# Weight parts of the token mixer made by converting and accumulating transfers, and the meta keys' rests stacked into one value product

## The chip, the cores and the metric

The kernel runs on one core of one Trainium2 chip, in one launch. The metric is the device time of an execution in microseconds. Engines are called by their names in the profile: PE (TensorE matmul) and PEld (its weight loads), DVE (VectorE), ACT (ScalarE), POOL or Pool (GpSimd), SP (SyncE, which here only issues transfers).

## What is computed

One decoder layer on 512 tokens of width 1024 with 16 meta tokens in front: half a SwiGLU FFN (inner width 2816), a token mixer, another half FFN. The reference, cut to the mixer:

```python
def token_mixer(h, ...):
    qa, ka, va, fa, qb, kb, vb, ga, gb = jnp.split(h @ w_in, idx, axis=-1)
    # qa, ka: rms_norm per head (8 heads of 64); qb 8 heads, kb, vb 2 heads, normed too
    log_f = jax.nn.log_sigmoid(fa + forget_bias)
    o_fox = fox_attention(qa, ka, va, log_f)       # causal, + c_q - c_k with c = cumsum(log_f)
    o_swa = swa_attention(qb, kb, vb, sinks, rel_bias_table)
    # each query block of 128 sees its own block, the block before and the 16 meta keys
    y = sigmoid(ga) * (o_fox @ w_branch_fox) + sigmoid(gb) * (o_swa @ w_branch_swa)
    return y @ w_out
```

## The kernel before

**Products in two parts.** Every fp32 operand of a large product is split into a leading part in fp32r (names ending in H, or `wh`) and the rest (L, or `wl`). `prod` (lines 301 to 304) makes one product of three matmuls: leading by leading, leading by rest, rest by leading.

**Weights.** Weights are read in pieces of 128x1024 (512 KB), in the fixed order of the list `pieces`. `load_to` has SP transfer a piece into a buffer `raw`; `split_to` then has ACT cast it into `wh` (`hi`, line 133) and DVE write the rest `wl = raw - wh` (`lo`, line 140). Each of the names `raw`, `wh`, `wl` has three buffers. `piece()` hands out the next piece; it keeps five pieces loaded ahead and three split ahead. The FFNs and the gates' last part use products with sums of weights instead (pieces of kinds A to D), some of which Pool's accumulating transfers make (line 211, `raw` and `rawC` from `in_w1i`, `in_wg` and others, 256 KB each).

**The mixer** (361.6 to 601 us of the profile). The projection is cut into nine chunks of 256 columns with two pieces each (rows 0 to 511 and 512 to 1023 of the weight): first v of the first four fox heads together with the forget gate, then k, q of the same heads, v, k, q of the other four, then k and v of the sliding window, then its two q chunks. Then come three gate pieces `wg` and four pieces `wbr` of the branch product, another gate piece, and the rest. `tok_chunk` makes a chunk for five token tiles (tile 0 is the 16 meta tokens, whose H and L stand side by side in `xm`, so that lines 1009 and 1010 take two matmuls instead of three). For k and q, `head_norm` takes ACT's squares, DVE's sums and a reciprocal root on Pool (`rsq`, line 351), then DVE scales, PE transposes (line 1139) and ACT and DVE evacuate into `kH`, `kL`, `qH`.

**Attention.** Units of attention are woven between the steps of the chunks that come later, so that PE always has projections to do while DVE and ACT work on a softmax; a scheduler then fixes the order on each engine. A fox unit takes two heads and 256 queries: scores (line 1221) with DVE's pass over them (line 1240), exponentials on ACT (line 1181), transposes (line 1266), evacuation into `pH` and `pL`, and value products (lines 1280 and 1281): for each key tile one matmul with `pH` and one with `pL`. Its stationary side `v` carries the leading part and the rest of v side by side in 128 columns, so one product gives both. Tile 0 of the keys holds the 16 meta keys in rows 0 to 15; rows 16 to 127 of that block of `v` are zero. A sliding-window unit takes four heads and one block of 128 queries: scores with the bias added on DVE (`tensor_tensor_reduce`, L1375 in the profile), exponentials, transposes (line 1388) per key tile, and value products (lines 1399 and 1400). Blocks 1 to 3 have three key tiles there, block 0 two: the meta keys (a tile of 16 rows) and its own block.

Of the kernel before, what the change touches and what calls it, by code (L numbers as in the profile page):

```python
# [41 lines left out]
TH = T // 2  # L42

# [39 lines left out]
def kernel(  # L83
# [117 lines left out]
    state = {"use": 0, "load": 0, "split": 0}  # L201
# [36 lines left out]

    def load_to(n):
        while state["load"] < min(n, holds[0] if holds else n, len(pieces)):  # L240
            c = state["load"]
            state["load"] += 1
            kind, *what = pieces[c]
            if kind == "w":
                parts = what[0]
                nk = parts[0][1]
                w = sum(p[2] for p in parts)
                raw = wp.tile([P, PW], F32, tag="raw", name=nm("raw"))
                rv = raw[:, : nk * w].rearrange("p (k c) -> p k c", c=w)
                c0 = 0  # L250
                for ap, _, n_ in parts:
                    SP.dma_start(rv[:, :, c0 : c0 + n_], ap)
                    c0 += n_
                raws[c] = (raw[:, : nk * w], nk, w)
            elif kind == "A":
                raws[c] = load_first(*what)
            elif kind == "B":
                raws[c], raws[c + 1], raws[c + 2] = load_others(*what)
# [5 lines left out]
    def split_to(n):  # L264
        while state["split"] < min(n, len(pieces)):
            c = state["split"]
            load_to(c + 1)
            state["split"] += 1
            raw = raws.pop(c)
            if callable(raw):  # L270
# [12 lines left out]

    def piece(ahead=None, then=None):

        c = state["use"]
        state["use"] += 1
        if then is not None and c in split:
            then(split[c])
            then = None  # L290
        split_to(c + (ahead or state["ahead"]))
        load_to(c + 5)
        if then is not None:
            then(split[c])
        return split.pop(c)

# [732 lines left out]
    def tok_chunk(alloc, tiles, evac, finish=None):  # L1029
# [3 lines left out]
        def one(i, half):  # L1033
# [45 lines left out]

    def v_evac(v, i, src):  # L1080
# [5 lines left out]
        lo(d[:, :, 1], src, d[:, :, 0], r1[:n, i : i + 1])  # L1086

# [105 lines left out]
    def fox_pair(box, p, ip, before):  # L1193
# [60 lines left out]
        def turn(hh):  # L1254
            for gr in [list(range(j, min(j + 2, nt))) for j in range(0, nt, 2)]:
# [13 lines left out]
                hi(pH[:, a:b], ps[:, a:b])  # L1269
                lo(pL[:, a:b], ps[:, a:b], pH[:, a:b])  # L1270

        def values(hh):
# [3 lines left out]
            for j in range(nt):  # L1276
# [4 lines left out]
                PE.matmul(pv[:, a:256], st, pL[:, c0 + a : c0 + 256], start=False, stop=j == nt - 1)  # L1281
# [65 lines left out]
    def swa_unit(box, qbox, g, i, before):  # L1347
# [6 lines left out]
        tiles = [(0, M, P), (1, P, 0)] if i == 0 else [(i, P, 0), (0, P, P), (i + 1, P, KS)]  # L1354

        def scores():
            before()
            q, k, b1 = qbox["q"], box["k"], b1s[g]
            for hp in range(2):
                t2 = new("t", [P, 546], F32, 4)  # L1360
                for hh in (2 * hp, 2 * hp + 1):
# [10 lines left out]
                        [(0, P, b1[:, hh, KS:]), (P, KS, bm0[:, h])] if i == 0 else [(0, nk, b1[:, hh])]  # L1372
                    )
                    for pi, (a, b, bt) in enumerate(bias):
                        V.tensor_tensor_reduce(  # L1375
                            out=t[:, a:b], in0=ps[:, a:b], in1=bt, scale=-0.125, scalar=init,
# [7 lines left out]
        def turn():  # L1384
            for tt, n, c0 in tiles:
                ps = psum()
                for hh in range(4):
                    PE.transpose(ps[:n, P * hh : P * hh + P], ts_[hh][:, c0 : c0 + n], ident)  # L1388
                pH, pL = new("pH", [P, 512], bufs=3), new("pL", [P, 512], bufs=3)
                hi(pH[:n], ps[:n])  # L1390
                lo(pL[:n], ps[:n], pH[:n])
                pts.append((pH, pL))

        def values():
            v = box["v"]
            pv = psum()
            for j, ((tt, n, c0), (pH, pL)) in enumerate(zip(tiles, pts)):
                st = v[:n, tt, P * g : P * g + P]
                PE.matmul(pv, st, pH[:n], start=j == 0, stop=False)
                PE.matmul(pv, st, pL[:n], start=False, stop=j == len(tiles) - 1)  # L1400
# [8 lines left out]
    def feat_steps(wsrc, srcH, srcL, nk, c0, use, cuts=4, w=S, whole=False):  # L1409
# [3 lines left out]
        def part(j):  # L1413
            if j == 0:
                box["w"] = wsrc()
                box["ps"] = psum(whole)
            wH, wL = box["w"]
# [19 lines left out]
    w0 = [piece(), piece()]  # L1437
    ps0 = [psum() for _ in every]
    for k in range(KD):
        for i in every:  # L1440
# [116 lines left out]
    stM.close()  # L1557

# [361 lines left out]
```

## Time and profile before

| | us |
|---|---|
| median of 3 runs | 1080.73 (1080.53 to 1080.74) |
| span of the profiled execution | 1078.4 |
| first FFN, mixer, rest of the gates and second FFN | 361.6, 239.4, 477.4 |
| busy in the span: PE, PEld | 1069.1 (99%), 1037.1 (96%) |
| busy in the span: DVE, ACT, POOL | 891.8 (83%), 656.5 (61%), 196.2 (18%) |

The profile is one execution; its span runs from the first to the last instruction, and 2.3 us of the run's time lie outside it. Matmuls overlap, so the time that one costs is the distance between the starts of two neighbours and not its own duration. In a row of the timeline stand the start, the duration, engine, line, operation, output<-inputs and shape, and in brackets how long the engine had been idle before it and what ended that.

### The profile page before, as it was taken

What the parts mean: (1) busy time and instruction counts of PE and PEld (TensorE: products, weight loads), DVE (VectorE), ACT (ScalarE), POOL (GpSimd) and SP (SyncE); (2) the same over time, 40 slices, a digit from 0 to 9 for tenths busy, and PEclk for the clock granted to TensorE, in tenths of its full rate; (3) what the DMA queues carried; (4) which work ended last, traced back from release to release, by engine and by line L of the source; (5) the groups of instructions that cost most, each with busy time, mean ns of one, the idle gap of its engine ahead of it and who ended that gap; (6) DMA issues with size and microseconds to landing.
All of it is one profiled execution on the core that took longest, in us unless ns stands there. A gap on an engine that the chain in (4) does not pass through costs nothing.

```text
span 1078.4 us, 22338 instructions
## 1 busy us (share of the span) xinstructions
PE 1069.1 (99%) x8587; PEld 1037.1 (96%) x8587; DVE 891.8 (83%) x1718; ACT 656.5 (61%) x1243; POOL 196.2 (18%) x232
## 2 busy tenths in 40 slices
PE   8999999999999999999999999999999999999998
PEld 8999999999999999999887799999999999999998
DVE  7988878888889577788897799788998788887895
ACT  7667456656666455556667866555666466645664
POOL 3011111121124431221200110001122211221120
PEclk9999999999999999999999999999999999999999
DMA  8787778688776423112211765466688877887753
GB/s 280 199 220 161 191 190 197 153 219 213 183 177 171 121 81 118 54 47 81 80 50 50 234 165 149 172 200 197 175 204 164 201 192 179 178 194 193 161 122 104
DMA packets 111723, 173.06 MB, mean 160 GB/s; under 512 B 10800, under 2 KB 58160, under 8 KB 111232
## 3 DMA queue, kind: packets, MB, share of 16 engines
q1 hardware_dynamic: 74032, 122.03, 35.5%
q0 software_dynamic: 28768, 37.83, 22.7%
q10 hardware_dynamic: 8816, 11.77, 3.4%
q8 instruction: 67, 1.10, 0.4%
q14 instruction: 40, 0.33, 0.1%
HBM read 167.37 MB, written 6.32 MB: 161 GB/s over the span
## 4 chain that ended last, share of the span: by engine, by line
PE 92%; DVE 3%; ACT 3%; issue 1%; DMA 0%; POOL 0%; SPq 0%; ACTq 0%; DVEq 0%
PE ps L301 16%; PE ps L304 15%; PE ps L302 15%; PE pt L301 13%; PE pt L302 13%; PE pt L304 13%; ACT t L1181 1%; ACT wh L133 1%; DVE wl L140 1%; PE pt L1221 1%; PE pt L1266 1%; DMA xt<-in_x_dram 0%; PE ps L1388 0%; DVE t L1184 0%; PE ps L1221 0%
## 5 line engine op out<-in xcount | busy, mean ns | idle before, releaser
L301 PE MATMUL ps<-x,wh 128*128 128x256 f32 (+2 forms) x768 | 219.7, 286 | 0.1
L302 PE MATMUL ps<-x,wh 128*128 128x256 f32 (+2 forms) x768 | 218.9, 285 | 0.5 <-DVE x L142 0.4
L304 PE MATMUL ps<-x,wl 128*128 128x256 f32 (+2 forms) x768 | 218.9, 285 | 0.0
L140 DVE TENSOR_TENSOR wl<-raw,wh 128x1024 fp32r<-128x1024 f32 (+3 forms) x125 | 150.0, 1201 | 44.4 <-ACT wh L133 43.1
L133 ACT CAST wh<-raw 128x1024 fp32r<-128x1024 f32 (+3 forms) x125 | 128.5, 1029 | 88.9 <-PE ps L302 58.3
L301 PEld LDWEIGHTS ps<-x,wh 128*128 128x128 f32 x768 | 144.7, 189 | 1.7 <-ACT hT L686 0.3
L302 PEld LDWEIGHTS ps<-x,wh 128*128 128x128 f32 x768 | 144.5, 188 | 1.4 <-DVE x L142 0.9
L304 PEld LDWEIGHTS ps<-x,wl 128*128 128x128 f32 x768 | 144.6, 188 | 0.8
L301 PE MATMUL pt<-x,wh 128*128 128x256 f32 (+2 forms) x424 | 125.3, 297 | 0.2 <-ACT wh L133 0.2
L304 PE MATMUL pt<-x,wl 128*128 128x256 f32 (+2 forms) x424 | 124.5, 294 | 0.0
L302 PE MATMUL pt<-x,wh 128*128 128x256 f32 (+2 forms) x392 | 112.5, 287 | 0.0
L133 ACT CAST wh<-tc 128x1024 fp32r<-128x1024 f32 (+1 forms) x70 | 71.9, 1026 | 64.5 <-DVE tc L234 57.1
L140 DVE TENSOR_TENSOR wl<-tc,wh 128x1024 fp32r<-128x1024 f32 (+1 forms) x70 | 83.5, 1193 | 32.5 <-ACT wh L133 32.2
L301 PE MATMUL ps<-acts,wh 128*128 128x264 f32 (+1 forms) x352 | 100.5, 285 | 0.1
L304 PE MATMUL ps<-acts,wl 128*128 128x264 f32 (+1 forms) x352 | 99.9, 284 | 0.0
L302 PE MATMUL ps<-acts,wh 128*128 128x264 f32 (+1 forms) x352 | 99.5, 283 | 0.0
L140 DVE TENSOR_TENSOR wl<-rawC,wh 128x1024 fp32r<-128x1024 f32 (+1 forms) x70 | 84.2, 1203 | 5.8 <-ACT wh L133 5.5
L133 ACT CAST wh<-rawC 128x1024 fp32r<-128x1024 f32 (+1 forms) x70 | 71.6, 1023 | 22.8 <-PE pt L302 17.8
L301 PEld LDWEIGHTS pt<-x,wh 128*128 128x128 f32 x424 | 79.9, 189 | 2.6 <-ACT wh L133 0.5
L304 PEld LDWEIGHTS pt<-x,wl 128*128 128x128 f32 x424 | 79.7, 188 | 2.1
L302 PEld LDWEIGHTS pt<-x,wh 128*128 128x128 f32 x392 | 73.8, 188 | 0.6
L301 PEld LDWEIGHTS ps<-acts,wh 128*128 128x128 f32 x352 | 66.5, 189 | 0.7 <-DVE h2T L918 0.3
(424 smaller groups left out, 3251.0 us busy)
## 6 DMA issues: line engine op xcount, KB each, us to landing
rawC<-in_w1i_dram SPq DMA_DIRECT2D x20, 512.0 KB, 4.6
raw<-in_w1i_dram SPq DMA_DIRECT2D x40, 256.0 KB, 4.2
raw<-in_w2i_dram SPq DMA_DIRECT2D x40, 256.0 KB, 3.4
rawC<-in_w2i_dram SPq DMA_DIRECT2D x20, 512.0 KB, 4.4
raw<-in_wm_dram SPq DMA_DIRECT2D x18, 512.0 KB, 4.4
raw<-in_wout_dram SPq DMA_DIRECT2D x16, 512.0 KB, 4.0
rawD<-in_w1i_dram SPq DMA_DIRECT2D x20, 256.0 KB, 4.1
raw<-in_w1i_dram POOLq DMA_DIRECT2D x20, 256.0 KB, 5.1
```

The costliest lines, as they stand in the source:

```text
L133: return A.copy(o, i)
L140: return V.tensor_tensor(out=o, in0=i, in1=h, op=ALU.subtract)
L301: PE.matmul(ps, sH, mH, start=first, stop=False, **more)
L302: PE.matmul(ps, sH, mL, start=False, stop=False, **more)
L304: shared["mm"] = PE.matmul(ps, sL, mH, start=False, stop=last, **more)
L1181: shared["exp"] = A.activation(t, t, AF.Exp, bias=nmx, scale=-1.0, accum_out=l[:, j : j + 1])
L1221: PE.matmul(ps[:, :w], q[qx][hb, hp, P * i : P * i + P], k[kx][hb, hp, c0 : c0 + w], start=qx + kx == 0, stop=qx == 1 and not last,)
L1266: PE.transpose(ps[:, c : c + P], ts_[hh][(c // P) % 2][:, c0 : c0 + P], ident)
```

## The change

**Weights.** 23 pieces become a new kind "m": the sixteen of the chunks behind the first, the first three of `wg` and the four of `wbr[0]`. For these, `load_to` calls `round_by_dma`, a transfer on Pool's queue that converts f32 to fp32r on its way into `wh`. `split_to` calls `rest_by_dma`: ACT writes `wl = -wh`, and a second transfer of the same weights on Pool's queue is added into `wl`. SP no longer loads these pieces, ACT no longer casts them and DVE no longer subtracts. Every fourth such piece takes two `raw` buffers in place of a `wh` and a `wl`. In the mixer, four pieces are loaded and two split ahead, and `pump` starts the second transfers at fixed places in a chunk.

**Meta keys.** Pool copies the meta rows of `v` also into rows 32 to 47 of the same block, and DVE writes the rest of the meta keys' probabilities into rows 32 to 47 of `pH`, so that one value product takes both; the product with `pL` goes for tile 0. The first block of the sliding window takes its meta keys at the front of the tile with its sink column, with 128-row transposes and products as in the other blocks.

```diff
+    def round_by_dma(ap, nk, w):
+
+        tags = ("raw", "raw") if made[0] % 4 == 3 else ("wh", "wl")
+        made[0] += 1
+        wh, wl = (wp.tile([P, PW], F32R, tag=t, name=nm("m" + t)) for t in tags)
+        wh, wl = (t[:, : nk * w].rearrange("p (k c) -> p k c", c=w) for t in (wh, wl))
+        G.dma_start(wh, ap)
+        return ap, wh, wl
+
+    def rest_by_dma(ap, wh, wl):
+
+        A.activation(wl, wh.bitcast(F32), AF.Copy, scale=-1.0)
+        G.dma_start(wl, ap, accum_op=ALU.add)
+        return wh, wl
...
-            pieces.append(("w", [(wm[c][:, k : k + 4, :], 4, 256)]))
+            pieces.append(("w" if c == 4 else "m", [(wm[c][:, k : k + 4, :], 4, 256)]))
-    pieces += [("w", [(wg[m], 8, 128)]) for m in range(NG - 1)]
-    pieces += [("w", [(wbr[0, c], 4, 256)]) for c in range(4)]
+    pieces += [("m", [(wg[m], 8, 128)]) for m in range(NG - 1)]
+    pieces += [("m", [(wbr[0, c], 4, 256)]) for c in range(4)]
...
         split_to(c + (ahead or state["ahead"]))
-        load_to(c + 5)
+        load_to(c + state["room"])
...
+    def pump():
+        split_to(state["use"] + 2)
...
+            if half and i == tiles[1]:
+                pump()
...
+    def meta_rest(p, ps, w):
+
+        lo(p[REST : REST + M, :w], ps[:M, :w], p[:M, :w])
+
...
+        if i == 0:
+            w = d.shape[1] * 2 * HD
+            G.tensor_copy(v[REST : REST + M, 0, :w], v[:M, 0, :w].bitcast(F32))
...
+                if gr[0] == 0:
+                    meta_rest(pH, ps, 256)
+                    a = 256
                 lo(pL[:, a:b], ps[:, a:b], pH[:, a:b])
...
-                PE.matmul(pv[:, a:256], st, pL[:, c0 + a : c0 + 256], start=False, stop=j == nt - 1)
+                if j:
+                    PE.matmul(pv[:, a:256], st, pL[:, c0 + a : c0 + 256], start=False, stop=j == nt - 1)
...
-        tiles = [(0, M, P), (1, P, 0)] if i == 0 else [(i, P, 0), (0, P, P), (i + 1, P, KS)]
+        tiles = [(0, 0), (1, M + 1)] if i == 0 else [(i, 0), (0, P), (i + 1, KS)]
...
     w0 = [piece(), piece()]
+    state.update(mix=True, room=4, ahead=2)
+    load_to(state["use"] + 2)
...
     stM.close()
+    state.update(room=5, ahead=3)
```

In the built program PE has 24 matmul rows fewer, POOL 49 rows more, SP 23 fewer. Line numbers of the rows below are those of the kernel they are from.

POOL at the start of the mixer, before: the last small loads, then memsets of `v` and `qn`, and the reciprocal root for v.

```order
L967 DMA bm0_4863<-biasd_142 128x8x16
L968 DMA gq_4871<-in_gqk_dram 128x4
L969 DMA fb_4872<-in_fbias_dram 128x8
L970 DMA snk_4873<-in_sinks_dram 128x8
L1100 MEMSET v_692_4896 128x512
L1126 MEMSET qn_718_5105 128x256
L1100 MEMSET v_770_5430 128x512
L351 TENSOR_TENSOR r1_4890<-r1_4890,nhalf_83 128x5
```

The same place after the change (`mwh` and `mwl` are the two parts of a piece made by transfers; `mwh_693` with `mwl_694` and `mwh_695` with `mwl_696` are the two pieces of the first k chunk):

```order
L1000 DMA snk_4869<-in_sinks_dram 128x8
L254 DMA mwl_694_4899<-in_wm_dram 128x1024
L1139 MEMSET v_690_4892 128x512
L1165 MEMSET qn_714_5099 128x256
L248 DMA mwh_695_4901<-in_wm_dram 128x1024
L1139 MEMSET v_764_5424 128x512
L254 DMA mwl_696_4902<-in_wm_dram 128x1024
L248 DMA mwh_706_5068<-in_wm_dram 128x1024
L381 TENSOR_TENSOR r1_4886<-r1_4886,nhalf_83 128x5
```

The converting transfer of the second piece now stands behind two memsets, its accumulating one behind a third, and the root behind both and behind the next chunk's first transfer.

ACT around the evacuation of the second fox group's q (`qH`), before: squares for head norms (`hsq`), a cast of a piece, probabilities (`pH`), then `qH`.

```order
L1061 ACTIVATE hsq_946_6283<-pt_938_6242 128x256
L133 CAST wh_953_6310<-raw_892_6020 128x1024
L1094 COPY hsq_949_6297<-ps_948_6290 64x256
L1025 COPY hsq_960_6339<-pt_959_6322 16x256
L133 CAST pH_965_6353<-ps_964_6352 128x512
L133 CAST pH_968_6362<-pt_967_6361 128x512
L1061 ACTIVATE hsq_962_6344<-hsq_960_6339 16x128
L133 CAST pH_971_6371<-ps_970_6370 128x128
L134 ACTIVATE qH_889_6015<-ps_974_6390,gq_4871 128x512
```

And after the change, where L253 is the negating copy:

```order
L1093 ACTIVATE hsq_934_6273<-pt_926_6231 128x256
L1133 COPY hsq_937_6286<-ps_936_6280 64x256
L253 ACTIVATE mwl_883_6014<-mwh_882_6013 128x1024
L1055 COPY hsq_946_6324<-pt_945_6307 16x256
L134 CAST pH_951_6339<-ps_950_6338 128x512
L1093 ACTIVATE hsq_948_6329<-hsq_946_6324 16x128
L134 CAST pH_954_6349<-pt_953_6348 128x512
L134 CAST pH_957_6358<-ps_956_6357 128x128
L253 ACTIVATE mwl_942_6300<-mwh_941_6299 128x1024
L135 ACTIVATE qH_879_6007<-ps_960_6377,gq_4867 128x512
```

One cast ahead of these steps became two negations, one ahead of five of them and one right ahead of `qH`.

More of the change, by code (lines that the diff above doesn't have):

```diff
@@ L42 @@
 TH = T // 2
+REST = 32
 def bc(ap, pos, n):
@@ L200 @@
     xm_place = lambda n: cp.tile([P, KD * P], F32R, tag="xm", name=nm(n))
-    state = {"use": 0, "load": 0, "split": 0}
+    state = {"use": 0, "load": 0, "split": 0, "room": 5, "mix": False}
     shared = {}
@@ L237, in load_others @@
         return sums, (c[:, : 2 * w], 2 * n, 128), (d[:, :w], n, 128)
+    made = [0]
+    def round_by_dma(ap, nk, w):
[9 more added lines that the diff above has]
+        return wh, wl
     def load_to(n):
@@ L241, in load_to @@
             c = state["load"]
+            if pieces[c][0] == "m" and not state["mix"]:
+                return
             state["load"] += 1
             kind, *what = pieces[c]
-            if kind == "w":
+            if kind == "m":
+                raws[c] = round_by_dma(*what[0][0])
+            elif kind == "w":
                 parts = what[0]
@@ L266, in split_to @@
             c = state["split"]
+            if pieces[c][0] == "m" and not state["mix"]:
+                return
             load_to(c + 1)
@@ L269, in split_to @@
             raw = raws.pop(c)
+            if pieces[c][0] == "m":
+                split[c] = rest_by_dma(*raw)
+                continue
             if callable(raw):
@@ L1384, in turn @@
         def turn():
-            for tt, n, c0 in tiles:
+            for tt, c0 in tiles:
                 ps = psum()
                 for hh in range(4):
[L1388 to L1391, printed above, removed]
+                    PE.transpose(ps[:, P * hh : P * hh + P], ts_[hh][:, c0 : c0 + P], ident)
+                pH, pL = new("pH", [P, 512], bufs=3), None
+                hi(pH, ps)
+                if tt:
+                    pL = new("pL", [P, 512], bufs=3)
+                    lo(pL, ps, pH)
+                else:
+                    meta_rest(pH, ps, 512)
                 pts.append((pH, pL))
@@ L1396, in values @@
             pv = psum()
[L1397 to L1400, printed above, removed]
+            for j, ((tt, c0), (pH, pL)) in enumerate(zip(tiles, pts)):
+                st = v[:, tt, P * g : P * g + P]
+                PE.matmul(pv, st, pH, start=j == 0, stop=False)
+                if tt:
+                    PE.matmul(pv, st, pL, start=False, stop=j == len(tiles) - 1)
             pvv = pv.rearrange("p (a b q) -> p a b q", b=2, q=P)
@@ L1416, in part @@
                 box["ps"] = psum(whole)
+            elif j == 1:
+                pump()
             wH, wL = box["w"]
```

8 lines of the change are left out of this document (5 added, 3 removed).

## Prediction

> **What bounds the kernel now.** I read the busy times by stage first (per engine PE, PEld, DVE, ACT, POOL, then clock, DMA share, GB/s; 361.60 to 601.00 us is the mixer, the stretch that the change touches), then the chain of waits by engine.
>
> ```profile
> 361.60:601.00 239.40, 237.26 (x1819) 216.02 (x1818) 186.00 (x536) 141.59 (x342) 41.68 (x57) 1.00 0.24 75
> 601.00:1078.40 477.40, 473.19 (x3855) 465.56 (x3853) 401.01 (x674) 287.91 (x500) 77.52 (x79) 1.00 0.71 179
> sum 1078.40, PE 1069.13 PEld 1037.10 DVE 891.80 ACT 656.50 POOL 196.18; mean PE 356.38 PEld 345.70 DVE 297.27 ACT 218.83 POOL 65.39
> ```
>
> ```profile
> PE 92%; DVE 3%; ACT 3%; issue 1%; DMA 0%; POOL 0%; SPq 0%; ACTq 0%; DVEq 0%
> ```
>
> PE is busy for 1069 of 1078.4 us and carries 92% of the chain; in the mixer it is idle for 239.40 - 237.26 = 2.1 us, at a full clock (1.00). So there are two ways to move the time: fewer matmuls (a gain at once), or a new wait of PE (a loss at once, since there is hardly any idle time to absorb it). DVE (186.0 of 239.4) and Pool (41.7) have room; time taken from them counts only where PE waits for them. The profiled execution spans 1078.4 us and the median of the runs is 1080.73, so 2.3 us lie outside the span; I add them to every result.
>
> **The matmuls that go.** Sixteen value products of fox (256 columns) and eight of the sliding window (512 columns) disappear. In the timeline of PE before:
>
> ```profile
> 511.36 0.28 PE L1280 MATMUL ps<-pH,v 128*128 128x256 f32 x1
> 511.48 0.28 PE L1281 MATMUL ps<-pL,v 128*128 128x256 f32 x1
> ...
> 538.20 0.50 PE L1399 MATMUL pt<-pH,v 16*128 16x512 f32 x1
> 538.54 0.38 PE L1400 MATMUL pt<-pL,v 16*128 16x512 f32 x1
> 538.86 0.50 PE L1399 MATMUL pt<-pH,v 128*128 128x512 f32 x1
> 539.19 0.39 PE L1400 MATMUL pt<-pL,v 128*128 128x512 f32 x1
> 539.42 0.60 PE L1139 MATMUL ps<-ident,qn 128*128 128x128 f32 x4
> ```
>
> Durations overlap, so a matmul's price is the distance between starts: 0.12 us for 256 columns (511.36 to 511.48), 0.23 for 512 columns in a full stream (539.19 to 539.42). Fox: 16 x 0.12 = 1.9. Of the sliding window's eight units, the six with three key tiles lose one product of 0.23 each: 1.4. The two units of the first block have four products now, 538.20 to 539.42 = 1.22 us, where 16-row and 128-row stationary operands alternate and three of the starts are 0.32 to 0.34 apart; three full-height ones at 0.23 would take 0.69, so 0.53 each, 1.1. Together **-4.4**. The rests of the meta probabilities have 16 rows instead of up to 128, so DVE writes them in no more time, and Pool's three small copies of v have its idle time to hide them.
>
> **The subtractions and casts that go.** Groups by line in the mixer:
>
> ```profile
> L140 DVE TENSOR_TENSOR wl<-raw,wh 128x1024 fp32r<-128x1024 f32 x23 | 28.0, 1219 | 5.6 <-ACT wh L133 5.6
> L133 ACT CAST wh<-raw 128x1024 fp32r<-128x1024 f32 x23 | 24.1, 1050 | 10.6 <-PE pt L304 4.8 <-PE pt L302 2.5 <-PE ps L304 1.8
> ```
>
> DVE loses 23 x 1.22 = 28 us. ACT loses no time: a negating copy of the same size stands for each cast, so I price it at 1.05. DVE's 28 us matter only where a subtraction stood in front of something that PE waits for. The clearest place, DVE first and then PE:
>
> ```profile
> 508.17 1.23 DVE L140 TENSOR_TENSOR wl<-raw,wh 128x1024 fp32r<-128x1024 f32 x1 [0.59 <-ACT wh L133]
> 509.31 0.57 DVE L1240 CUSTOM_DVE_ANT_0 t<-ps,cb 128x400 f32<-128x400 f32 x1
> ```
>
> ```profile
> 509.75 0.28 PE L301 MATMUL pt<-wh,x 128*128 128x256 f32 x1
> 510.44 0.39 PE L1221 MATMUL pt<-kH,qH 64*128 64x264 f32 x1 [0.41 <-DVE nmx L1240]
> ```
>
> The score pass follows the subtraction at once; without it PSUM comes free sooner, and what is over the usual distance before 510.44 goes (0.69 - 0.12): **-0.6**. Anything from 0 to the mixer's whole idle time (2.1) is possible. Gains: 4.4 + 0.6 = **5.0**.
>
> **What is added: a chain of two Pool transfers per piece.** A piece now goes: PE releases the buffer; Pool issues the converting transfer; it lands; ACT negates; Pool issues the accumulating transfer; it lands; PE may use the rest. No row of before shows either transfer at this size. The nearest, from the list of DMA issues (KB each, median us from issue to landing), and the two queues (packets, MB, share of 16 engines):
>
> ```profile
> raw<-in_wg_dram POOLq DMA_DIRECT2D x6, 256.0 KB, 4.6
> ...
> h2T<-h1d POOLq DMA_DIRECT2D x1, 512.0 KB, 4.4
> ```
>
> ```profile
> q1 hardware_dynamic: 74032, 122.03, 35.5%
> q0 software_dynamic: 28768, 37.83, 22.7%
> ```
>
> The first accumulates, the second is a plain copy. A MB of SP's queue costs 0.355 x 1078.4 x 16 / 122.03 = 50 us of one DMA engine, and a MB of Pool's (mostly accumulating) 0.227 x 1078.4 x 16 / 37.83 = 103. So 256 KB more of accumulation on 16 engines add about 1.6 to the 4.6, if nothing overlaps. I take 5.5 for an accumulation of 512 KB (4.6 to 6.6) and 4.9 for the converting transfer (4.4, as plain, to 5.4, dearer or beside another).
>
> *At the start of the k chunk*, the first chunk made in this way. Pool's new order puts the second piece's converting transfer behind the two memsets:
>
> ```profile
> 368.92 0.53 POOL L1100 MEMSET v<- 128x512 f32 x1 [0.64 <-PE pt L304]
> 369.38 0.31 POOL L1126 MEMSET qn<- 128x256 f32 x1
> ```
>
> ```profile
> 377.57 0.28 PE L1010 MATMUL pt<-wl,xm 128*128 128x256 f32 x1
> ```
>
> It starts at 369.7 to 369.9 and lands at 374.8; ACT's negation ends 1.05 later, at 375.9; the accumulation starts at 376.2 and lands at 381.7. PE first used the rest of this piece at 377.57; three matmuls are now ahead of it (3 x 0.12), so it is wanted at 377.9. Stall: **+3.8** (369.7 + 4.4 + 1.05 + 4.6 = 379.8 gives 1.9; 369.9 + 5.4 + 1.05 + 0.6 of turns + 6.6 = 383.5 gives 5.6). Behind this accumulation on Pool stand the third piece's transfer and the reciprocal root for v; ACT's scaling of v waits for that root, and the stall covers both.
>
> By the Trainium skill, "DMA: Bandwidth & Descriptors", section "Anatomy of one DMA — SWDGE (gpsimd) path", a transfer on this path takes about 2.0 us plus its bytes over 436 GB/s, as an estimate 3.2 us for 512 KB, by which the second rest would land near 377.3 and nothing would stall. The row of 4.4 for the plain 512 KB speaks against it here.
>
> *ACT in front of qH*: the second fox group's q is evacuated while the first piece of the sliding window's q chunk is made. The timelines of Pool, ACT and PE:
>
> ```profile
> 460.54 1.01 POOL L351 TENSOR_TENSOR hss<-hss,nhalf 128x4 f32<-128x4 f32 x1 [2.59 <-DVE hss L1063]
> ```
>
> ```profile
> 465.45 0.36 ACT L1025 COPY hsq<-pt 16x256 f32<-16x256 f32 x1 [0.64 <-PE pt L1010]
> ...
> 467.06 0.24 ACT L133 CAST pH<-ps 128x128 fp32r<-128x128 f32 x1
> 469.17 0.69 ACT L134 ACTIVATE qH<-ps,gq 128x512 fp32r<-128x512 f32 x1 [1.87 <-PE ps L1139]
> ```
>
> ```profile
> 469.91 0.38 PE L1221 MATMUL ps<-kH,qH 64*128 64x256 f32 x1
> ```
>
> Pool comes to the converting transfer after the root, at 461.5; it lands near 466.2 and the negation ends near 467.3 at the latest, 467.1 with a landing at 466.0; the five ACT steps that began at 465.45 (to 467.30, 1.85) now begin there (end 468.95), and with a second negation (1.05) behind them ACT comes to qH at 470.0 instead of 469.17; PE used qH at 469.91. Stall **+0.9** (0.2 if the transfer lands at plain price, 2.0 if 1 us later).
>
> *ACT between the exponentials of a sliding-window unit.* A piece's cast stood at 561.79, before four exponentials (0.40 each); its negation has to wait for a landing first. ACT, DVE, PE:
>
> ```profile
> 561.79 1.06 ACT L133 CAST wh<-raw 128x1024 fp32r<-128x1024 f32 x1 [1.57 <-PE ps L302]
> ...
> 565.97 0.40 ACT L1181 ACTIVATE t<-t,nmx 128x145 f32<-128x145 f32 x1
> ```
>
> ```profile
> 566.71 0.71 DVE L1184 TENSOR_SCALAR t<-t,l 128x145 f32<-128x145 f32 x3
> ```
>
> ```profile
> 568.50 0.60 PE L1388 MATMUL ps<-ident,t 128*16 128x128 f32 x4
> ```
>
> Release near 561.7 plus 4.5 is 566.2, where two exponentials were still to come by the new order; negation to 567.3, two exponentials to 568.2, DVE's scaling 1.0 behind them (565.97 + 0.5 to 567.42 before) to 569.2, against 568.50: **+0.7** (0, landing before 564.7, to 2.0).
>
> *The other boundaries.* The k chunk's last use of its first buffers, and the start of the second v chunk, which needs their successors:
>
> ```profile
> 389.58 0.28 PE L304 MATMUL pt<-wh,x 128*128 128x256 f32 x1
> ...
> 402.73 0.28 PE L1009 MATMUL ps<-wh,xm 128*128 128x256 f32 x1
> ```
>
> That leaves 13 us and more (the second piece is wanted 0.9 later, the first is released 1.4 earlier: about 14 each) for a chain of 4.9 + 1.05 + 5.5 = 11.5 and the turns before it on Pool and ACT, about 1. Nine such boundaries have between 1 and 20 us to spare; I take **+1.3** for all (0 to 4.0, the latter about 0.45 at each). Whatever stands on Pool behind a transfer that waits for PE's release, reciprocal roots mainly, waits too; what hides that is the time between a head norm and its transposes.
>
> Sum: -5.0 + 3.8 + 0.9 + 0.7 + 1.3 = +1.7; 1078.4 + 1.7 + 2.3 = **1082.4 us**. With the unknowns not all at one end, this case alone reaches from 1080 to 1086.
>
> **The rivals.** *The transfers land in time.* Needed at the k chunk: both together in 377.9 - 369.9 - 1.05 = 7.0 us, where the rows give 9.0 or more. For it: DMA engines are 24% busy in the mixer, and the row of 4.6 comes from the stretch behind it, at 71%. Then about 0.7 is left at all places: 1080.7 - 5.0 + 0.7 = 1076.4, faster. The skill's rule above would give this; no row yet shows a transfer that short. *Only the first stall is real,* small work of ACT and Pool finding room at the later places: 1080.7 - 5.0 + 3.8 + 0.5 = 1080.0, no change. Against it: both run their rows in a fixed order, so a row that waits blocks those behind it. *The chain is at its upper bounds everywhere:* the converting transfer costs what an accumulating one does. From a chain longer than the 14 us on, every boundary stalls: 5.6 + 2.0 + 2.0 + 4.0 - 5.0 = +8.6, so 1089.3, clearly slower.
>
> **How the numbers follow.** About 0.2% (2.2 us: 1078.6 to 1082.9) is what a measurement of this kernel can tell from no change. The forecast gets 0.46, of which its bounds put 0.24 above 1082.9 and 0.22 below; transfers in time 0.20 (faster); only the first stall 0.14 (same); the upper bounds 0.20 (slower). So faster 0.20, same 0.36, slower 0.44. The range, 1077 to 1088, cuts off about half of the first rival's chance and half of the last one's.
>
> **What would show it.** Right: PE idle between about 377.9 and 382, ended by a DMA into the rest of the k chunk's second piece; accumulations of 512 KB landing after 5 to 6 us; the first scores after 470 late behind qH; 24 matmuls fewer, and DVE's busy time down by about 25 us. Wrong: no wait of PE for a DMA at 378; landings of 3.5 us or less, or of 8 and more; PE waiting for Pool's roots instead; or value products whose starts do not close up by 0.12 and 0.23.

## The result and the profile after

The changed kernel took 1097.01 us (median; 1093.18 to 1097.73) against 1080.74 in the same comparison: a ratio of 1.0142, 95% interval 1.0128 to 1.0155. It is 16.3 us slower where 1.7 were forecast, outside the range. Among its four runs the time falls as the mean granted clock rises: 1097.73, 1097.21, 1096.82 and 1093.18 us at 0.991, 0.992, 0.995 and 0.997. The profiled execution spans 1095.3 us. The page's busy times and its chain of waits:

```profile
span 1095.3 us, 22331 instructions
...
PE 1074.8 (98%) x8563; PEld 1040.9 (95%) x8563; DVE 871.5 (80%) x1711; ACT 656.5 (60%) x1243; POOL 230.9 (21%) x281
...
PE 82%; DVE 6%; DMA 4%; ACT 4%; issue 3%; POOL 1%; ACTq 0%; SPq 0%; POOLq 0%; DVEq 0%
```

The busy times by stage (same columns as before; the third last column is the granted clock):

```profile
361.60:617.90 256.30, 242.84 (x1797) 219.53 (x1796) 165.24 (x529) 142.15 (x343) 74.39 (x104) 0.97 0.50 118
617.90:1095.30 477.40, 473.19 (x3852) 465.64 (x3850) 401.13 (x674) 287.31 (x500) 76.71 (x79) 1.00 0.71 178
```

The stretch behind the mixer takes 477.40 us as before, so the whole difference, 256.3 - 239.4 = 16.9 us, lies in the mixer. PE's idle time there went from 2.1 to 256.30 - 242.84 = 13.5 us, and PE is *also* busy for 5.6 us longer (242.84 against 237.26), although it has 24 matmuls fewer (22 by the counts of the rows, in which a few records are missing). DVE lost 20.8 us, which is not seen as time. PE's waits in 360 to 620 us (total, times, longest):

```profile
PE pt L1040 <- DMA mwl<-in_wm_dram: 4.5, 1, 4.5
PE pt L1178 <- DVE qn L1105: 3.5, 3, 1.6
PE ps L1260 <- ACT qH L135: 1.8, 1, 1.8
PE ps L1178 <- DVE qn L1105: 1.4, 1, 1.4
```

The first row is the forecast's first stall. In PE's timeline there:

```profile
377.79 0.28 PE L334 MATMUL ps<-mwh,x 128*128 128x256 f32 x1
382.57 0.58 PE L1040 MATMUL pt<-mwl,xm 128*128 128x256 f32 x1 [4.50 <-DMA mwl<-in_wm_dram]
382.95 0.42 PE L1039 MATMUL pt<-mwh,xm 128*128 128x256 f32 x1
383.16 0.42 PE L1040 MATMUL pt<-mwl,xm 128*128 128x256 f32 x1
```

Look at the starts behind the wait: 0.21 us apart, where a matmul of 256 columns took 0.12. The wait is not the whole price. The same place, and the one around 421 us, in windows cut at the changes of the clock:

```profile
377.10:380.50 3.40, 0.96 (x9) 0.76 (x7) 1.20 (x8) 0.73 (x3) 2.64 (x3) 1.00 0.49 72
380.60:383.90 3.30, 1.33 (x6) 1.33 (x7) 1.36 (x5) 0.62 (x2) 0.60 (x1) 0.50 0.83 238
383.90:387.30 3.40, 3.40 (x18) 3.40 (x18) 1.89 (x5) 2.79 (x5) 0.92 (x1) 0.50 0.00 0
387.40:390.80 3.40, 3.40 (x31) 3.40 (x30) 1.43 (x7) 3.34 (x6) 0.18 (x1) 1.00 0.84 148
```

```profile
401.00:404.40 3.40, 1.87 (x18) 1.52 (x16) 1.71 (x5) 2.98 (x7) 2.54 (x3) 1.00 0.30 47
418.10:421.50 3.40, 1.56 (x16) 1.37 (x14) 0.69 (x2) 2.42 (x4) 0.87 (x1) 1.00 1.04 265
421.50:424.90 3.40, 3.22 (x20) 2.51 (x19) 3.40 (x12) 1.57 (x6) 0.60 (x1) 0.50 1.05 178
424.90:428.30 3.40, 3.40 (x18) 3.40 (x18) 2.00 (x8) 1.83 (x7) 0.00 (x0) 0.50 0.13 25
```

PE is idle for about 2.4 us of the first window, and from 380.5 to 387.35 it is granted half its clock: 18 matmuls in 3.4 us instead of 31. The same happens from 421.5 to 428.3, and from 486.35 to 489.8. Against the usual spacing the starts in these three stretches lose about 2.0, 2.9 and 1.7 us, 6.6 together. The stretches are 6.8, 6.8 and 3.4 us long, and their beginnings lie 41.0 and 64.9 us apart, 12 and 19 times 3.41 us.

How two of the other waits arise, the one of 1.5 us near 403 and the one of 1.8 at 421. First ACT and then DVE near 400:

```profile
396.80 0.39 ACT L1093 ACTIVATE hsq<-pt 128x256 f32<-128x256 f32 x1 [2.44 <-PE pt L334]
400.50 1.06 ACT L253 ACTIVATE mwl<-mwh 128x1024 fp32r<-128x1024 f32 x1 [3.32 <-DMA mwh<-in_wm_dram]
401.46 0.37 ACT L1093 ACTIVATE hsq<-ps 128x256 f32<-128x256 f32 x1
```

```profile
401.86 0.42 DVE L1094 TENSOR_REDUCE hss<-hsq 128x4 f32<-128x256 f32 x1 [3.58 <-ACT hsq L1093]
402.32 0.23 DVE L1095 TENSOR_SCALAR hss<-hss,r1sq 128x4 f32<-128x4 f32 x1
402.45 0.48 DVE L1105 SCALAR_TENSOR_TENSOR qn<-pt,r,hss 128x256 f32<-128x256 f32 x1
```

ACT's negation waits 3.32 us for a converting transfer to land; the squares of the *next* q tile stand behind it, DVE's sum of them behind these, and the scaling of the last k tile (`qn`), whose root on Pool was done at 399.1, behind that sum. PE waits for that scaling. Near 421, ACT again:

```profile
419.04 1.06 ACT L253 ACTIVATE mwl<-mwh 128x1024 fp32r<-128x1024 f32 x1 [6.10 <-DMA mwh<-in_wm_dram]
420.12 0.36 ACT L1055 COPY hsq<-ps 16x256 f32<-16x256 f32 x1
420.50 0.69 ACT L135 ACTIVATE qH<-ps,gq 128x512 fp32r<-128x512 f32 x1
```

This transfer, issued at 410.98, took 8.04 us to land, the longest of those into `wh`: two loads of the forgetting sums (`cb`, 528 KB each on ACT's queue), a second conversion and an accumulation ran beside it. Which of these made it long was not tested. The list of DMA issues (medians; the `mraw` row holds conversions and accumulations together):

```profile
mwh<-in_wm_dram POOLq DMA_DIRECT2D x12, 512.0 KB, 4.8
mwl<-in_wm_dram POOLq DMA_DIRECT2D x12, 512.0 KB, 6.3
...
mraw<-in_wm_dram POOLq DMA_DIRECT2D x8, 512.0 KB, 7.2
...
cb<-cbd ACTq DMA_DIRECT2D x4, 528.0 KB, 6.3
```

### The profile page after: what moved, and what is told of

Its sections match the earlier page's. It is cut to its first block, busy times and chain, and to the rows that moved or that the text cites. A ratio compares the mean times of both kernels' runs of the same rounds, so it can differ in the third digit from the quotient of the medians.

```text
span 1095.3 us, 22331 instructions
## 1 busy us (share of the span) xinstructions
PE 1074.8 (98%) x8563; PEld 1040.9 (95%) x8563; DVE 871.5 (80%) x1711; ACT 656.5 (60%) x1243; POOL 230.9 (21%) x281
## 4 chain that ended last, share of the span: by engine, by line
PE 82%; DVE 6%; DMA 4%; ACT 4%; issue 3%; POOL 1%; ACTq 0%; SPq 0%; POOLq 0%; DVEq 0%
PE ps L331 14%; PE ps L332 14%; PE ps L334 14%; PE pt L331 11%; PE pt L332 11%; PE pt L334 11%; DMA mwh<-in_wm_dram 2%; DVE wl L141 1%; ACT wh L134 1%; DMA h1d<-hT 1%; PE ps L1431 1%; DMA mwl<-in_wm_dram 0%; DMA xt<-in_x_dram 0%; DMA mwh<-in_wg_dram 0%; DVE acts L460 0%
## 5 line engine op out<-in xcount | busy, mean ns | idle before, releaser
L332 PE MATMUL ps<-x,wh 128*128 128x256 f32 (+1 forms) x752 | 213.0, 283 | 0.5 <-DVE x L143 0.4
L331 PE MATMUL ps<-x,wh 128*128 128x256 f32 (+1 forms) x752 | 212.9, 283 | 0.2
L334 PE MATMUL ps<-x,wl 128*128 128x256 f32 (+1 forms) x752 | 212.7, 283 | 0.0
L141 DVE TENSOR_TENSOR wl<-raw,wh 128x1024 fp32r<-128x1024 f32 (+3 forms) x102 | 122.3, 1200 | 38.2 <-ACT wh L134 36.8
L134 ACT CAST wh<-raw 128x1024 fp32r<-128x1024 f32 (+3 forms) x102 | 104.3, 1025 | 73.2 <-PE ps L332 54.5
L331 PEld LDWEIGHTS ps<-x,wh 128*128 128x128 f32 x752 | 141.8, 189 | 0.9 <-ACT hT L716 0.3
L332 PEld LDWEIGHTS ps<-x,wh 128*128 128x128 f32 x752 | 141.5, 188 | 1.0 <-DVE x L143 0.9
L334 PEld LDWEIGHTS ps<-x,wl 128*128 128x128 f32 x752 | 141.9, 189 | 0.1
L331 PE MATMUL pt<-x,wh 128*128 128x256 f32 (+2 forms) x416 | 122.1, 294 | 0.3 <-ACT wh L134 0.3
L334 PE MATMUL pt<-x,wl 128*128 128x256 f32 (+2 forms) x416 | 121.5, 293 | 0.0
L332 PE MATMUL pt<-x,wh 128*128 128x256 f32 (+2 forms) x384 | 109.3, 285 | 0.0
L331 PEld LDWEIGHTS pt<-x,wh 128*128 128x128 f32 x416 | 78.5, 189 | 2.2 <-ACT wh L134 0.5
L332 PEld LDWEIGHTS pt<-x,wh 128*128 128x128 f32 x384 | 72.3, 188 | 0.4
```

The lines of the kernel that those rows point to most:

```text
L134: return A.copy(o, i)
L141: return V.tensor_tensor(out=o, in0=i, in1=h, op=ALU.subtract)
L331: PE.matmul(ps, sH, mH, start=first, stop=False, **more)
L332: PE.matmul(ps, sH, mL, start=False, stop=False, **more)
L334: shared["mm"] = PE.matmul(ps, sL, mH, start=False, stop=last, **more)
```

## The experiments

The theory after the result: each chain of release, conversion, negation and accumulation needs more time than a chunk leaves it; ACT and Pool, which have to wait inside the chain, hold up the head norms behind them; and PE pays for each wait twice, first its length and then some microseconds of half clock. The rivals: a wait costs its length only; the stacking of the meta keys brought waits of its own; one early accident (the order of Pool's memsets) sets off the rest.

**The two halves apart.** First the stacking alone: all pieces stay of kind "w" and are loaded as far ahead as before (first block of the diff, against the changed kernel; only its first lines are shown). Then the transfers alone: value products and tiles as before (second block, also cut).

```diff
-            pieces.append(("w" if c == 4 else "m", [(wm[c][:, k : k + 4, :], 4, 256)]))
+            pieces.append(("w", [(wm[c][:, k : k + 4, :], 4, 256)]))
...
-                if gr[0] == 0:
-                    meta_rest(pH, ps, 256)
-                    a = 256
...
-                if j:
-                    PE.matmul(pv[:, a:256], st, pL[:, c0 + a : c0 + 256], start=False, stop=j == nt - 1)
+                PE.matmul(pv[:, a:256], st, pL[:, c0 + a : c0 + 256], start=False, stop=j == nt - 1)
```

> Only the stacked meta keys; all weights as before. Theory: the 24 value products that go are worth 4.4 us by their starts and nothing new is waited for, so 1076.3 us (1075.5 to 1077.5). Rival: the small copies and the reordered tiles of the sliding window bring waits of their own, so that part of the loss sits here: 1079 us or more.

> Only the weights' parts made by transfers; meta keys as before. Theory: the whole loss comes from here, and the two parts add up: the changed kernel's 1097.0 plus the 4.4 us of the stacking, 1101 us (1098 to 1104). Rival: the parts interact, the stacking's reordering causing some of the waits: 1097 us or less.

The stacking alone took 1081.59 us, ratio 1.0011 (1.0002 to 1.0020): the rival, no gain at all. The transfers alone took 1094.83 us, 1.0142 (1.0127 to 1.0158), the same ratio as the whole change. The 1101 us expected for them were missed, since there was no gain of the stacking to take away: 1.2 us for it and 14.4 for the transfers, each against the kernel before of its comparison, make 15.6 of the 16.3. So the loss is the transfers', and the stacking adds about 1 us at most, which is at the edge of what can be told. The kernel with the transfers alone is at half clock at the first of the three places only (380.6 to 387.4), and loses nearly as much; the share of the clock in the loss differs from kernel to kernel, and waits are the larger part of it. The stacking's products did get shorter: from start to next start, all value products together cost 26.7 us before and 22.5 now, 4.2 less (4.4 had been forecast). But eight transposes now give 128 rows instead of 16, the transposes of these units cost 1.1 us more in all, and waits were added (0.60 us near 492 and 1.34 at 518). The largest, DVE and then PE of this kernel:

```profile
517.61 0.41 DVE L141 TENSOR_TENSOR pH<-ps,pH 16x256 fp32r<-16x256 f32 x1
518.05 0.42 DVE L141 TENSOR_TENSOR pL<-ps,pH 128x256 fp32r<-128x256 f32 x1
```

```profile
518.08 0.51 PE L1322 MATMUL ps<-pH,v 128*128 128x256 f32 x2 [1.34 <-DVE pH L141]
```

A unit's first value product reads the rows that DVE has just added, so it waits for DVE, where before it needed only ACT's cast. And two DVE passes (0.41 and 0.42) stand where one of 0.68 stood.

**The first stall, three ways.** The k chunk's pieces by SP, as before; then 36 extra matmuls in the gap; then the raw buffers for the second, sixth, ... piece in place of the fourth, eighth, ..., since they are free earlier.

```diff
-            pieces.append(("w" if c == 4 else "m", [(wm[c][:, k : k + 4, :], 4, 256)]))
+            pieces.append(("w" if c in (4, 2) else "m", [(wm[c][:, k : k + 4, :], 4, 256)]))
...
+            if k == 4 and width == 256 and pads:
+                for _ in range(pads.pop()):
+                    PE.matmul(ps[:, 256:512], xm[:, 0], w[0][0][:, 0], start=True, stop=True, skip_group_check=True)
...
-        tags = ("raw", "raw") if made[0] % 4 == 3 else ("wh", "wl")
+        tags = ("raw", "raw") if made[0] % 4 == 1 else ("wh", "wl")
```

> The changed kernel, but the two pieces of the first k chunk loaded by SP, cast and subtracted as before. Theory: PE's wait of 4.5 us at 378 goes, and with it the half clock from 380.5 to 387.4, which cost 2.1 us more; 1097.0 - 6.6 = 1090.4 us (1088 to 1092.5), unless another place falls behind instead. Rival (a wait costs its length alone): 1097.0 - 4.5 = 1092.5 or more. Both expect the waits near 403 and 421 to stay, since they come from the chunks behind.

> The changed kernel with 36 matmuls more of 256 columns, into unused columns of PSUM that nothing reads, ahead of the matmul that waits at 378; PE stays busy for 36 x 0.12 = 4.2 us of the 4.5 us wait, and nothing else changes. Theory (the half clock follows from the idle time): the clock stays full at 380 to 388, and the kernel gets 2.1 us faster, 1095 us, although it does more work. Rival (the slower spacing after the wait has another cause, such as transfers or late weights): spacing stays 0.21 there, time unchanged or up, 1097 us or more.

> The changed kernel with the pair of raw buffers given to the second, sixth, ... of the new pieces in place of the fourth, eighth, ...: the k chunk's second piece then has buffers that are free early, so its converting transfer is queued some 8 us earlier. Theory: the wait at 378 with its half clock goes (6.6 us) and the waits further on, which come from releases and from ACT's order, stay: 1090.5 us (1088 to 1093). Rival: as with the k chunk loaded by SP, the wait moves to the next chunk, whose pieces now take the late buffers, and half or more of the loss stays: 1093 us or more.

With the k chunk by SP the kernel took 1090.53 us, 1.0095 (1.0081 to 1.0109), the number expected, but not in the way expected: the wait at 378 is gone, and new ones stand at 394.8 and 401.6, with a half clock from 395.8 to 399.2. The edit does a second thing: every fourth new piece takes the raw buffers, and as the count now starts two pieces later, other pieces get them; how much of the new waits comes from that was not tested. Its two longest waits of PE:

```profile
PE ps L331 <- DMA mwh<-in_wm_dram: 2.5, 1, 2.5
PE pt L1178 <- DVE qn L1105: 1.5, 1, 1.5
```

The 6.5 us gained are as much as the removed chunk's own stall had cost (4.5 and 2.0); 10.1 us of loss remain behind it. The kernel with the filled gap (its output differs, but its instructions are the same except for the 36) took 1099.42 us, 1.0173 (1.0160 to 1.0187). At the place itself the theory holds; PE's timeline there:

```profile
377.92 4.46 PE L1044 MATMUL pt<-mwh,xm 128*128 128x256 f32 x36
382.86 0.39 PE L1045 MATMUL pt<-mwl,xm 128*128 128x256 f32 x1 [0.48 <-DMA mwl<-in_wm_dram]
383.08 0.28 PE L1041 MATMUL pt<-mwh,xm 128*128 128x256 f32 x1
383.20 0.28 PE L1045 MATMUL pt<-mwl,xm 128*128 128x256 f32 x1
```

PE was kept busy, the starts behind are 0.12 apart, and behind it PE has lost 5.0 us against the kernel before, instead of 6.9. But reaching the next chunk earlier made it wait there longer, 2.9 us for `qn` near 403 in place of 1.5, now with a half clock from 402.9 to 406.3; near 530 the waits for `qn` are 3.3 in place of 2.0. The row of its waits:

```profile
PE pt L1183 <- DVE qn L1110: 6.3, 3, 2.9
```

The time that was expected of the whole kernel, 1095, was missed. The trace is of its quickest run, 1096.49 us at a mean clock of 0.998; the three others took 1099.17 to 1100.97 at 0.994 and 0.995, and where these lost the clock no trace shows. The raw buffers for other pieces did not help either: 1096.84 us, 1.0144 (1.0128 to 1.0159), the rival. No wait at 378, and near 400:

```profile
399.30 1.06 ACT L253 ACTIVATE mwl<-mwh 128x1024 fp32r<-128x1024 f32 x1 [5.92 <-DMA mwh<-in_wm_dram]
400.27 0.37 ACT L1093 ACTIVATE hsq<-ps 128x256 f32<-128x256 f32 x1
```

```profile
401.79 0.47 PE L1178 MATMUL pt<-ident,qn 128*128 128x128 f32 x1 [5.70 <-DVE qn L1105]
```

So the first stall does not set off the rest: with it removed or filled, waits stand at the chunks behind, and in the last two kernels what was saved at 378 was lost there again.

**One wait by itself.** The kernel before, with only the second piece of the k chunk made by transfers (and with the changed kernel's loading ahead, four pieces loaded and two split; away from this piece its waits of PE over 0.25 us in the mixer are those of the kernel before, about 0.4 each).

```diff
-            pieces.append(("w", [(wm[c][:, k : k + 4, :], 4, 256)]))
+            pieces.append(("m" if (c, k) == (2, 4) else "w", [(wm[c][:, k : k + 4, :], 4, 256)]))
```

> The kernel before with one piece, the second of the first k chunk, made by transfers, nothing else; its converting transfer stands behind the memsets. It measures one wait by itself. Its length by the rows of the changed kernel: 4 to 6 us. Theory (the clock halves during the wait and costs half of the 5 to 7 us behind it): the kernel is slower by the wait and 1.5 to 2.5 us more, 1087.5 us (1086 to 1090), with a clock of 0.5 behind the wait. Rival (a wait costs its length): slower by the wait alone, and the spacing behind it stays 0.12.

It took 1085.80 us (1084.71 to 1086.90), 1.0043 (1.0028 to 1.0059), 0.2 under the range expected. PE in its profile (of the run of 1086.44 us):

```profile
381.48 0.58 PE L1040 MATMUL pt<-mwl,xm 128*128 128x256 f32 x1 [3.52 <-DMA mwl<-in_wm_dram]
381.86 0.41 PE L1039 MATMUL pt<-mwh,xm 128*128 128x256 f32 x1
382.08 0.41 PE L1040 MATMUL pt<-mwl,xm 128*128 128x256 f32 x1
```

The wait was shorter than expected (3.5 us, not 4 to 6): with no other new transfer beside it the conversion landed in 4.0 us, where it took 5.7 in the changed kernel. From the end of that stretch to the end of the kernel PE is 6.2 us late: the wait of 3.5 and about 2.5 of half clock, 0.21 from start to start until 387. So a wait was paid twice here too, where little else changed; over the four runs the price beyond 3.5 us is 0.4 to 2.6.

**Who has to wait in the chain.** The negation on Pool in place of ACT; then, with the raw buffers as above, ACT's negations behind the squares of the chunk's first tile. The second edit also splits one piece ahead instead of two and starts the second transfers after a tile's evacuation instead of before it; these lines are not shown.

```diff
-        A.activation(wl, wh.bitcast(F32), AF.Copy, scale=-1.0)
+        G.tensor_scalar(wl, wh.bitcast(F32), -1.0, None, op0=ALU.mult)
...
+            if "sq" in shared:
+                st.enter_context(tc.issue_after(shared["sq"]))
+            A.activation(wl, wh.bitcast(F32), AF.Copy, scale=-1.0)
```

> The changed kernel with the negation on Pool in place of ACT. ACT then no longer waits for landings (23 us of such waits in the profile). If ACT's blocked row is what makes the head norms near 403 and qH near 421 late, those waits go, 5 to 8 us, against up to 4 us more at 378 (Pool's copy of this size, by its cast of half the size in 1.6 us, takes about 3 us): 1092 to 1096 us. If any engine that stands in the chain blocks its other rows in the same way (theory), Pool's reciprocal roots wait in place of ACT's squares, and with the longer chain the kernel is slower: 1099 to 1108 us.

> The kernel with the raw buffers given to the second, sixth, ... piece (1096.8 us, where the first wait of PE was 5.7 us for qn near 400), but with the negations that wait for a landing issued behind the squares of the chunk's first tile. Theory (ACT's row that waits for a landing holds up the squares behind it, and with them DVE's scaling of the last k tile): the wait for qn near 400 goes with the half clock behind it, some 7 us; the next weights come about 2 us late instead: 1091 us (1088 to 1093.5). Rival (the chain of transfers is late by itself, whatever ACT's order): PE waits for the next chunk's weights as long as it did for qn, 1095 us or more.

On Pool: 1115.11 us, 1.0315 (1.0301 to 1.0329), slower than the theory's own figure (1099 to 1108), and not by its mechanism: PE's waits for `qn` shrink to 0.7 us in all, so PE shows no head norm that is late behind Pool's roots. Pool's copy takes 2.8 us, PE waits for weights at four places, 19 us in all, and the clock is at half for 34 us of the mixer (17 in the changed kernel). With the squares first: 1099.40 us, 1.0165 (1.0151 to 1.0179), the rival. PE's waits in these two kernels, the first two rows of each:

```profile
PE pt L1040 <- DMA mwl<-in_wm_dram: 10.4, 2, 7.5
PE ps L1040 <- DMA mwl<-in_wm_dram: 8.6, 2, 8.1
```

```profile
PE ps L1045 <- DMA mwl<-in_wm_dram: 5.8, 1, 5.8
PE pt L1045 <- DMA mwl<-in_wm_dram: 5.7, 1, 5.7
```

The wait for `qn` near 400 went down to 0.9, as the theory had it, but the weights came later by as much, 5.8 us and not 2. The accumulation that PE waited for was issued at 401.86, 2.9 us after its negation began, and took 8.9 us to land beside loads of `cb`, conversions and another accumulation. So ACT's blocked row does hold up the head norms. That the chain has no time to give is what both kernels look like, but each changed more than the order on ACT, and it was not shown apart.

**What is left of the gain.** The stacking with the leading products of the other tiles first; the same with the seven late pieces made by transfers; the stacking in the sliding window alone with these seven; and that stacking with no transfers.

```diff
+            turns = [(j, 0) for j in (*range(1, nt), 0)] + [(j, 1) for j in range(1, nt)]
+            for n, (j, r) in enumerate(turns):
...
-            pieces.append(("w" if c == 4 else "m", [(wm[c][:, k : k + 4, :], 4, 256)]))
+            pieces.append(("w", [(wm[c][:, k : k + 4, :], 4, 256)]))
```

> Only the stacked meta keys, as in the first experiment (1081.6 us), with the value products in another order: the leading parts of the other key tiles first, then the meta tile's one product, then the rests. Theory: the stacking gained nothing because a unit's first product now reads rows that DVE writes and so waits for DVE (1.5 us at 518, 0.8 at 492), where before it needed only ACT's cast; with an ACT-only product first, most of these waits go and 2 to 3 us of the 4.4 come back: 1078.9 us (1077.5 to 1080). Rival: DVE's extra instruction per unit is late in any order, or the products' starts were never worth 4.4: 1081 us or more.

> The stacked meta keys in the new order, as in the experiment before the last, and of the pieces only the seven of the gates and the branch made by transfers, where releases come 20 us before use. Theory: no wait of PE for a weight there, and DVE's relief of 7 subtractions is worth little, so within 1 us of that experiment (1078 to 1080 us). Rival: even there the negation behind a landing blocks ACT between the exponentials, 2 us or more slower than that experiment.

> The stacking in the sliding window alone (eight products of 512 columns go, fox as before), and the seven late pieces made by transfers. Theory, by the shifts of the earlier experiments (fox gained nothing or lost 0.6, the sliding window gained 0.8 to 1.1): 1079.5 us (1078.8 to 1080.2), the fastest of all, by little. Rival: the gain of the sliding window was only the recovery of what fox had put off: 1080.4 us or more.

> The stacking in the sliding window alone, all weights cast and subtracted as before; the experiment before the last but one without its seven pieces made by transfers. If the gain there (1079.45 us against 1080.75) came from the eight products of 512 columns alone, it stays: 1079.5 us (1079 to 1080). If half or more of it came from the seven subtractions that DVE was spared (the difference of 1.0 us between the two experiments with the reordered products speaks for that): 1080.2 to 1081 us.

They took 1081.06 us, 1.0003 (0.9994 to 1.0012); 1080.07, 0.9993 (0.9984 to 1.0002); 1079.45, 0.9988 (0.9979 to 0.9997); and 1079.78, 0.9991 (0.9982 to 1.0000). The new order brought back 0.5 us by the medians and 0.8 against the comparison of each, not 2 to 3: the wait for the first product was real but not the main thing. In the profiles, counted from the mixer's first matmul with `xm`, fox's last value product comes 1.2 us later than before with fox stacked in the first order, 0.6 later in the new order (both kernels), and no later without fox's stacking; from there to the sliding window's last value product all five kernels take 0.3 to 0.7 us less. The late pieces did no harm; their rival, ACT blocked between exponentials, is not seen. The last kernel, 0.8 us shorter in the mixer (238.6 against 239.4), speaks for the eight products as the source of the small gain, which then needs no transfer:

```profile
361.60:600.20 238.60, 236.01 (x1810) 214.99 (x1809) 186.49 (x536) 141.57 (x342) 41.87 (x58) 1.00 0.24 75
```

The two last kernels are the only ones whose interval does not reach above the kernel before; they are 0.1% below it, which is at the edge of what can be told.

## Why the prediction was wrong

*The value products.* Sized rightly as matmuls (4.2 of 4.4), wrong as a gain: the stacking alone was 1.2 us slower. The step that failed is "DVE writes them in no more time": the meta rests are a second pass of 0.41 us per unit, and the first value product now waits for it. The forecast should have asked who writes each operand of the product that stays. But with that wait out of the way only 0.5 to 0.8 us came back, so this is a part of the loss of the gain and not all of it; where the rest of the 4.4 went stays open.

*DVE's relief* (-0.6). Not seen as time: DVE is 20.8 us less busy in the mixer. Seven subtractions fewer went with 1.0 us less where fox is stacked too (1081.06 to 1080.07) and 0.3 less where it is not (1079.78 to 1079.45); in both pairs the intervals overlap.

*The k chunk* (+3.8). The mechanism and the place were right: a wait of 4.5 us, ended by a DMA into the rest of the second piece; the conversion landed after 5.7, the accumulation after 5.4 (4.9 and 5.5 taken). What it lacked is the half clock behind it, 2.0 us more.

*ACT in front of qH* (+0.9). The place and the cause were right, the path was not. The negation waited for its landing and began at 479.90, and PE stopped for 1.43 us at 484.4, with 1.7 us of half clock behind it. But it stopped for `qn`, one step ahead of `qH`, and when ACT came to `qH` it was ACT that waited for PE:

```profile
484.42 0.33 PE L1178 MATMUL ps<-ident,qn 128*128 128x128 f32 x1 [1.43 <-DVE qn L1105]
```

```profile
484.78 0.69 ACT L135 ACTIVATE qH<-ps,gq 128x512 fp32r<-128x512 f32 x1 [1.04 <-PE ps L1178]
```

The mechanism as forecast, ACT late at `qH`, struck first at the first group's qH (1.84 us at 421, then 2.9 of half clock), which the forecast did not see since it took one landing time for all transfers; there the transfer had company and took 8.04.

*ACT between exponentials* (+0.7). Nothing at the place named: a negation does stand between the exponentials, near 583, but its landing was in time.

*The other boundaries* (+1.3). Too small: waits of 1.5 near 403 and 1.6 near 533 and smaller ones. "Whatever stands on Pool behind a transfer that waits for PE's release" named the wrong engine: near 403 it was ACT's squares. Near 533 `qn` stood behind DVE's scaling of the exponentials, and these, in a fox unit, behind a negation on ACT at 527.2; that this negation made them late was not tested.

The largest error runs through all of them: the step that failed most is the price of a wait. The working called a new wait of PE "a loss at once", counted each at its own length, and priced none of the half clock behind it: 6.6 of 16.9 us. Of the 15.2 us between the forecast and the mixer's 16.9, this is 6.6; the gains that did not come are about 5.0; and what is left, about 3.6, is waits that were longer than the 6.7 forecast. This last part is a remainder and no measurement. No row of the profile before could show the half clock, since PE never stops there for long. The Trainium skill, "TensorE: Matmul & The Clock Gate", section "Part 1: The HAM clock gate", says that the clock halves after an idle window of about 3.4 us and comes back after a busy one, the windows running freely. The trace agrees on the length and the fixed grid of the windows (3.41 us) and on the half rate; it differs in that 1.8 us of idle time within a window, and once 1.4, were enough, while 1.53 us near 402 were followed by no half clock, and in that a window busy for 3.22 of 3.40 us (421.5) did not bring the full clock back. What decides between 1.4 and 1.53 stays open. By that rule the forecast's first stall of 3.8 us could already have halved the clock; the working did not use it.

The rivals: the forecast's slowest, the chain at its upper bounds everywhere (+8.6), was nearest in number, and partly by luck. The accumulations into `wl` took 6.3 us (median), near its upper price of 6.6, but a conversion (4.8) did not cost what an accumulation does, and not every boundary stalled. Its 8.6 are 13.6 of stalls less 5.0 of gains; measured are 16.9 - 6.6 = 10.3 without the clock, and no gains. The rival of transfers in time fell with the first stall: the two transfers of that piece took 5.7 and 5.4 us, where 7.0 were there for both. That no row showed a transfer of 3.2 us holds for Pool's queue alone; the list of before has plain loads of 512 KB on SP's queue at 3.2 and 3.3 (`raw` from `in_w2i` and `in_wbr`). That only the first stall is real is refuted by the waits behind it.

## What to carry to other kernels

Where PE never waits, price a new wait at its length plus up to some 3 us of half clock (2.0, 2.9 and 1.7 here, and none behind two waits of 1.5 and 1.6), and work out for each new step which engine has to sit in front of it and what is queued behind that engine. A chain of release, transfer, copy and transfer again has to fit into the time between release and use with room for the slowest landing, not for the median; if it doesn't, curing one stall can just move it. Before a matmul is merged away, ask whether the operand that remains is ready as early as the one that it replaces; here that was a part of why nothing was gained.

## What the runs showed of the hardware

An accumulating transfer of 512 KB with little beside it landed in 5.4 us, a converting one in 3.5 to 4.3; with others beside them, up to 10.1 and 9.3. The half clock came and went on a grid of 3.41 us, and lasted for one or two steps of it in the changed kernel and for five at one place of the kernel that negates on Pool. The kernel with the single wait (3.5 us in its profile) was slower by 4.0 to 6.2 us from run to run: 1084.71 and 1085.16 us at a mean granted clock of 0.998, 1086.44 and 1086.90 at 0.996. A clock lower by 0.002 over 1085 us is some 2 us, so the clock accounts for most of the spread; that it comes from where the wait meets the grid was not tested.
